# Attention scores from 128-row blocks that hold a head's high query rows over its low rows

## The chip, the cores and the metric

The kernel runs on one core of one Trainium2 chip. A run's time is the device time of one execution in microseconds (us). The engines are named as in the profile: PE is the matrix engine (PEld its weight loads), DVE the vector engine, ACT the scalar engine, POOL the general engine, SP the one that issues most transfers.

## What is computed

Two layers, each of three steps with a layer norm behind every one: a gated feed-forward step, a mixer, and a second gated feed-forward step. Sequence 256, width 1024. The mixer of layer 0 is an mLSTM, that of layer 1 windowed attention with 16 query heads of 64 columns, 4 key heads, a distance bias and a sink logit per head. The change touches the attention alone, of which the reference is (cut):

```python
def window_attention(x, w_in, sink, w_out):
    p = x @ w_in
    ...
    s = jnp.einsum('bnqkgd,bnskd->bnkgqs', q, kw).astype(jnp.float32) * (HEAD_DIM ** -0.5)
    ...
    s = s - slopes[:, :, None, None] * dist
    s = jnp.where(valid[None, :, None, None], s, MASK_VALUE)
    ...
    m = jnp.maximum(jnp.max(s, axis=-1, keepdims=True), sink_l)
    pe = jnp.exp(s - m)
    attn = pe / (jnp.sum(pe, axis=-1, keepdims=True) + jnp.exp(sink_l - m))
    o = jnp.einsum('bnkgqs,bnskd->bnqkgd', attn, vw.astype(jnp.float32)).reshape(B, S, nq)
    return o.astype(x.dtype) @ w_out
```

## The kernel before

Every product of float32 matrices is made from two parts of each operand: a high part that PE multiplies in its own format, and a low part, what the high part leaves over. ACT writes the high part (a copy or an activation with a scale), DVE subtracts it from the source and writes the low part; `split_evac` does both for what PE left in PSUM. A product then takes three matmuls, high by high, high by low and low by high, added up in PSUM (`mm3`). Weights come in pieces of 128 x 1024, each split in the same way into the rings `w_hi` and `w_lo` of 10 buffers.

Attention (`attn`) goes as follows. `proj` makes keys, values and the first half of the queries by token; `k_turn` and `q_turn` transpose them on PE and evacuate them into `kk` and `q2`. The second half of the queries comes out of `q_rest` already transposed, in four tiles, interleaved with the first scores. `kk` holds each key head twice, in partitions 0 to 63 and 64 to 127. `q2[:, j]` holds the pair j of heads, one head in partitions 0 to 63, the other in 64 to 127, and the third index chooses the high or the low part.

There are 8 pairs of heads. For each pair j, `scores` makes, per 128 tokens t, three products of 64 rows for each of the two heads, alternating between the heads and between two PSUM banks. DVE adds the distance bias and takes the row's maximum (the score reduction, a custom operation that the profile shows as CUSTOM_DVE_ANT_0 and an accumulator read, and the order as ISA), ACT takes the exponential and its sum, and POOL divides (`scale`). One step later PE transposes the probabilities and they are split (`turn`: pr0 and pr1), then multiplied with the values (`values`). There ACT copies one product to `o` and DVE adds the other, which lies in the other half of the partitions: `nc.vector.tensor_add(o[top], p[low, 0], o[top])`, and the same for `o[low]`. The sum is split into `q2[:, j]`, whose queries are no longer needed, and `out_proj` multiplies it with the output weights. All that is interleaved over 11 steps `st`.

What is executed when is not this code's order. Each engine call is only recorded (`Engine`), and `Program.issue` (the line that the profile gives for nearly every instruction) emits the records in the order of a table of numbers, `ORDER`: each number is the distance to the next record. A second table, `SLOTS`, says which of its buffers each tile takes. Each engine works through its own instructions strictly in the order in which they are emitted.

Of the kernel before, what the change touches and what calls it, by code (L numbers as in the profile page):

```python
# [264 lines left out]
        "365018925167"),  # L265
    "t.0": ("10423251205145435305135232350"),
    "stats": ("101001110110"),
    "mv": ("011010011101"),
    "rs": ("100011011011"),
    "raw.1": ("12301301302312032103102130302130"),  # L270
    "wt.1": ("3210"),
# [165 lines left out]
def trunk_kernel(ctx: ExitStack, tc: tile.TileContext, x, ffn_w_in, ffn_w_out, ln_g, ln_b, ml_w_in, ml_gate_b,  # L437
                 ml_norm_g, ml_w_out, at_w_in, at_sink, at_w_out, out):
    nc = Program(tc.nc)
# [1047 lines left out]
```

## Time and profile before

| | us |
|---|---|
| three runs | 914.37, 915.44, 916.11 |
| median | 915.44 |
| span of the profiled execution, first to last instruction | 914.3 |
| first start of a score matmul | 670.1 |
| last start of a score matmul | 709.8 |

The profile gives the span alone of the execution that it took; it lies 1.1 us under the median of the runs and 0.1 under the fastest. Of the whole span, the scores of all heads take 39.7 us. A row of a view names the line, the engine, the operation, and what it writes and reads (output <- inputs, buffer numbers left out). `fp32r` is the format of the high and low parts. The timeline gives the start, the time from there to the end, and how many neighbours of one kind were put together (x2). On PE the instructions overlap: what one costs is the step to the next start.

### The profile page before, as it was taken

The page shows a single profiled execution, that of the slowest core. Times are in us where ns is not written, and L with a number is a line of the kernel's source. Part 1 is how long each engine was busy: PE and PEld are TensorE (multiplying, and loading weights), DVE is VectorE, ACT ScalarE, POOL GpSimd, SP SyncE. Part 2 cuts the span into 40 slices and gives each one's busy share as a digit, 9 for nine tenths or more (in the row PEclk, how much of TensorE's full clock was granted, in tenths as well). Part 3 has the DMA queues.
Part 4 walks back from the last instruction along what each step waited for, and adds up shares of the span by engine and source line. Part 5 has one row for each costly group of instructions (what it writes and reads, how often), then busy time and mean ns, then how long its engine had stood idle before and what let it go on. Part 6 is the DMA issues. An engine that isn't in the chain of part 4 may idle for free.

```text
span 914.3 us, 12376 instructions
## 1 busy us (share of the span) xinstructions
PE 903.8 (99%) x4382; PEld 748.2 (82%) x4382; DVE 812.8 (89%) x987; ACT 576.8 (63%) x796; POOL 156.8 (17%) x200
## 2 busy tenths in 40 slices
PE   9999999999999999999999999999999999999996
PEld 7888888889988888887888888888887788888885
DVE  6998989997798999888999988899899899988897
ACT  6667567557655677565747666666488557666560
POOL 0211112113311121111012111120435311202110
PEclk9999999999999999999999999999999999999999
DMA  9999889558273889898957899987543396997971
GB/s 334 299 298 298 246 248 240 180 179 263 94 260 114 270 252 256 269 280 197 341 196 188 229 277 296 277 178 259 173 173 116 116 277 166 257 303 174 321 182 46
DMA packets 100670, 208.52 MB, mean 228 GB/s; under 512 B 6872, under 2 KB 21232, under 8 KB 100608
## 3 DMA queue, kind: packets, MB, share of 16 engines
q1 hardware_dynamic: 82832, 173.83, 54.1%
q0 software_dynamic: 17632, 33.64, 22.4%
q8 instruction: 34, 0.56, 0.2%
q10 hardware_dynamic: 144, 0.26, 0.1%
q14 instruction: 28, 0.23, 0.1%
HBM read 206.65 MB, written 1.05 MB: 227 GB/s over the span
## 4 chain that ended last, share of the span: by engine, by line
PE 96%; DMA 2%; DVE 1%; issue 1%; ACT 0%; DVEq 0%; POOL 0%; POOLq 0%
PE p L317 96%; DMA s_raw<-in_ffn_w_in_dram 1%; DMA ln_g<-in_ln_g_dram 1%; DVE w_lo L317 0%; DVE x L317 0%; ACT w_hi L317 0%; DVE h_lor L317 0%; DVEq L1483 0%; DVE hc_lor L317 0%; DVE t L317 0%; ACT xT_hi L317 0%; DVE stats L317 0%; DVE mv L317 0%; POOL ji L317 0%; DVE ident L317 0%
## 5 line engine op out<-in xcount | busy, mean ns | idle before, releaser
L317 ACT CAST w_hi<-s_raw 128x1024 fp32r<-128x1024 f32 x239 | 244.5, 1051 | 94.5 <-PE p L317 56.4
L317 DVE TENSOR_TENSOR w_lo<-s_raw,w_hi 128x1024 fp32r<-128x1024 f32 x239 | 285.6, 1218 | 19.6 <-ACT w_hi L317 15.6
L317 ACT CAST w_hi<-w_raw 128x1024 fp32r<-128x1024 f32 (+1 forms) x167 | 172.1, 1041 | 77.9 <-PE p L317 37.6
L317 DVE TENSOR_TENSOR w_lo<-w_raw,w_hi 128x1024 fp32r<-128x1024 f32 (+1 forms) x167 | 199.8, 1208 | 14.5 <-ACT w_hi L317 13.3
L317 PE MATMUL p<-w_hi,xT_hi 128*128 128x512 f32 x512 | 191.9, 394 | 0.8 <-ACT w_hi L317 0.5
L317 PE MATMUL p<-w_lo,xT_hi 128*128 128x512 f32 x512 | 192.1, 394 | 0.0
L317 PE MATMUL p<-w_hi,xT_lo 128*128 128x512 f32 x512 | 191.3, 394 | 0.0
L317 PE MATMUL p<-w_hi,h_lor 128*128 128x512 f32 (+1 forms) x323 | 119.9, 390 | 0.1
L317 PE MATMUL p<-w_hi,h_hir 128*128 128x512 f32 (+1 forms) x323 | 119.5, 391 | 0.0
L317 PE MATMUL p<-w_lo,h_hir 128*128 128x512 f32 (+1 forms) x323 | 118.6, 389 | 0.0
L317 PEld LDWEIGHTS p<-w_hi,xT_hi 128*128 128x128 f32 x512 | 95.8, 188 | 20.4 <-ACT w_hi L317 1.0
L317 PEld LDWEIGHTS p<-w_lo,xT_hi 128*128 128x128 f32 x512 | 96.0, 188 | 19.5 <-DVE w_lo L317 0.4
L317 PEld LDWEIGHTS p<-w_hi,xT_lo 128*128 128x128 f32 x512 | 96.1, 188 | 19.3 <-DVE xT_lo L317 0.3
L317 POOL DMA_DIRECT2D s_raw<-in_ffn_w_in_dram x43 | 52.2, 1266 | 329.0 <-DVE w_lo L317 90.5
L317 PE MATMUL p<-w_hi,S_hir 128*128 128x512 f32 x256 | 96.9, 390 | 0.0
L317 PE MATMUL p<-w_hi,S_lor 128*128 128x512 f32 x256 | 96.8, 390 | 0.0
L317 PE MATMUL p<-w_lo,S_hir 128*128 128x512 f32 x256 | 96.8, 390 | 0.0
L317 PEld LDWEIGHTS p<-w_hi,h_lor 128*128 128x128 f32 x323 | 60.6, 188 | 12.6 <-DVE h_lor L317 0.5
L317 PEld LDWEIGHTS p<-w_lo,h_hir 128*128 128x128 f32 x323 | 60.7, 188 | 12.2
L317 PEld LDWEIGHTS p<-w_hi,h_hir 128*128 128x128 f32 x323 | 60.5, 188 | 12.3 <-ACT h_hir L317 0.2
L317 PEld LDWEIGHTS p<-w_hi,S_hir 128*128 128x128 f32 x256 | 48.0, 188 | 10.5 <-ACT t L317 0.4
L317 PEld LDWEIGHTS p<-w_lo,S_hir 128*128 128x128 f32 x256 | 48.1, 188 | 10.1 <-DVE w_lo L317 0.2
(187 smaller groups left out, 1176.7 us busy)
## 6 DMA issues: line engine op xcount, KB each, us to landing
s_raw<-in_ffn_w_in_dram SPq DMA_DIRECT2D x101, 512.0 KB, 6.0
w_raw<-in_ffn_w_in_dram SPq DMA_DIRECT2D x58, 512.0 KB, 6.3
s_raw<-in_ffn_w_out_dram SPq DMA_DIRECT2D x55, 512.0 KB, 5.8
s_raw<-in_ffn_w_in_dram POOLq DMA_DIRECT2D x43, 512.0 KB, 7.1
w_raw<-in_ffn_w_out_dram SPq DMA_DIRECT2D x33, 512.0 KB, 7.1
w_raw<-in_ml_w_in_dram SPq DMA_DIRECT2D x24, 512.0 KB, 5.2
w_raw<-in_ffn_w_in_dram POOLq DMA_DIRECT2D x21, 512.0 KB, 7.8
s_raw<-in_ffn_w_in_dram SPq DMA_DIRECT2D x20, 256.0 KB, 6.1
```

The lines of the kernel that those rows point to most:

```text
L317: f(*args, **kw)
```

## The change

The layout of `q2` is different. `q2[0:64, j, a]` now holds the high part of the head a of pair j, and `q2[64:128, j, a]` its low part: the high rows stand over the low rows. As `kk` holds each key head twice, one matmul of 128 rows with the high keys makes high by high and low by high at once, and one with the low keys high by low and low by low. A head and 128 tokens take two matmuls of 128 rows in place of three of 64 rows, and the product of the two low parts is now added too. Over 8 pairs, 2 heads and 2 halves of the tokens that is 64 matmuls in place of 96.

The evacuation of the queries is made per head, so that each of the six (two in `q_turn`, four in `q_rest`) is two of 64 partitions on ACT and two on DVE, where it was one of 128 on each. Half of them write other partitions than they read.

```diff
             def q_turn(t):
...
-                split_evac((q2[:, 0:4, 0, tok(t)], q2[:, 0:4, 1, tok(t)]), p)
+                for a in range(2):
+                    split_evac((q2[0:64, 0:4, a, tok(t)], q2[64:128, 0:4, a, tok(t)]), p[64 * a:64 * a + 64])
...
             def q_rest(part):
...
-                        split_evac((q2[:, j, 0], q2[:, j, 1]), p, qs_col[:, j - 4:j - 3])
+                        for a in range(2):
+                            r = slice(64 * a, 64 * a + 64)
+                            split_evac((q2[0:64, j, a], q2[64:128, j, a]), p[r], qs_col[r, j - 4:j - 3])
...
             def scores(j, between):
...
                 for t in range(2):
-                    for n_, (qe, ke) in enumerate(((0, 0), (0, 1), (1, 0))):
-                        for a in range(2):
-                            r = slice(64 * a, 64 * a + 64)
-                            nc.tensor.matmul(ps[a][:, t], q2[r, j, qe, tok(t)], kk[ke][r, g], start=n_ == 0, stop=n_ == 2)
+                    for a in range(2):
+                        for e in range(2):
+                            nc.tensor.matmul(ps[a][:, t], q2[:, j, a, tok(t)], kk[e][:, g], start=e == 0, stop=e == 1)
```

Only these places of the code are new, but the tables `ORDER` (6654 records before, 6634 now) and most of `SLOTS` are new throughout:

```diff
-    "0 10 -9 8 2 -9 11 -10 11 15 1 -26 11 1 -11 12 1 -12 13 12 -24 13 1 11 -10 1 1 1 1 1 8 -7 17 -37 28 10 1 72 "
...
-    "sc.4": ("4245315103514231504321"),
+    "sc.4": ("0152153014253012543012"),
```

Counted over the records that both versions have, the place of an instruction in its engine's order moves by 3 on PE in the median and by 64 at most; 599 of 949 on DVE stay at the same place, and none moves by more than 11.

PE's order at the scores of the last pair of heads, before (p is a PSUM bank, kk the keys, q2r the queries or, behind them, the attention's output, pr the probabilities, v the values, w the output weights):

```order
L317 MATMUL p4_92<-w_hi4_72,q2r_4_0_238 128x512
L317 MATMUL p6_94<-kk_hir_4_0_227,q2r_4_0_238 128x256
L317 MATMUL p7_95<-kk_hir_4_0_227,q2r_4_0_238 128x256
L317 MATMUL p6_94<-kk_lor_4_0_228,q2r_4_0_238 128x256
L317 MATMUL p6_94<-kk_hir_4_0_227,q2r_4_0_238 128x256
L317 MATMUL p7_95<-kk_lor_4_0_228,q2r_4_0_238 128x256
L317 MATMUL p7_95<-kk_hir_4_0_227,q2r_4_0_238 128x256
L317 MATMUL p3_91<-w_hi9_77,q2r_4_0_238 128x512
```

And now, at the same pair:

```order
L312 MATMUL p6_94<-w_hi5_73,q2r_4_0_238 128x512
L312 MATMUL p0_88<-kk_hir_4_0_227,q2r_4_0_238 128x256
L312 MATMUL p5_93<-pr0_hir_4_1_250,v0r_4_0_236 128x512
L312 MATMUL p0_88<-kk_lor_4_0_228,q2r_4_0_238 128x256
L312 MATMUL p0_88<-kk_hir_4_0_227,q2r_4_0_238 128x256
L312 MATMUL p0_88<-kk_lor_4_0_228,q2r_4_0_238 128x256
L312 MATMUL p5_93<-pr1_hir_4_0_253,v1r_4_0_237 128x512
```

Six matmuls of 64 rows that stood in one block, two banks in turn, have become pairs of one bank that other matmuls are put between.

DVE's order at two evacuations of `q_rest`, before (sc are the scores, o and pr as above, w_lo a weight's low part):

```order
L317 TENSOR_TENSOR pr1_lor_4_1_256<-p1_89,pr1_hir_4_1_254 128x512
L317 SCALAR_TENSOR_TENSOR q2r_4_0_238<-p6_94,qs_col_4_0_226,q2r_4_0_238 128x256
L317 SCALAR_TENSOR_TENSOR q2r_4_0_238<-p4_92,qs_col_4_0_226,q2r_4_0_238 128x256
L317 TENSOR_TENSOR o_4_0_257<-p0_88,o_4_0_257 64x256 x2
L317 ISA sc_4_4_233,nm_4_1_242<-p4_92,dist_4_0_235,neg_sink_151 128x256
```

And now, at the last of the four:

```order
L312 TENSOR_TENSOR pr1_lor_4_1_256<-p7_95,pr1_hir_4_0_253 128x512
L312 TENSOR_TENSOR w_lo5_83<-w_raw3_67,w_hi7_75 128x1024
L312 SCALAR_TENSOR_TENSOR q2r_4_0_238<-p6_94,qs_col_4_0_226,q2r_4_0_238 64x256 x2
L312 TENSOR_TENSOR q2r_4_0_238<-o_4_0_257,q2r_4_0_238 128x256
L312 TENSOR_TENSOR o_4_1_258<-p4_92,o_4_1_258 64x256 x2
```

Where one instruction evacuated a tile of queries, two stand next to each other (x2), of 64 partitions each.

More of the change, by code (lines that the diff above doesn't have):

```diff
@@ L39 @@
 ORDER = (
[208 rows of a table removed]
[205 rows of a table added]
 )
 SLOTS = {
-    "raw.0": ("210375894260ab315798a1b2380476593806142893750a61b4735a0286b12a940280"),
-    "p": ("3015273416371651624740737037743003470071732475045321703262751465120457615023462034756305172461503713"
-        "6442055504252022042555024574651034561742340220420324423044423643153426021762340152301647420765314722"
-        "060227602276670206205326743621306753342132312243113214236"),
+    "raw.0": ("9173029854a76b31208961b439750a28397a1549830276a1b50326749ab146857497"),
+    "p": ("4026415701530160147372353253735225372270652373467520345212370617024673107425612456371547012610547317"
+        "2006455540656466406555461530231470520316714664164761167411175403560345135274032105612704420351674033"
+        "253025252003523053231625460452037610045200520045225024057"),
@@ L254 @@
     "h_hir.0": ("01001"),
     "h_lor.0": ("10101"),
-    "w_hi": ("1536089427819056375820935612483172106249564780132954061782549302675180974325916874210359678241306597"
-        "8240637195824063718459026378591430268719546372150862437689061249085367241903758623104975268413908217"
-        "5469870321659748031256784901375628147093568273041695371208346897520134659782013465920871649356809217"
-        "5368049215063874921506387491206537891234706592318672398160257386541934670253891457260389415762058963"
-        "905268715496"),
@@ L261 @@
-    "w_lo": ("8138121742486951046580796125370164658235182350986541234970895268317504678250734095386210549378012564"
-        "3185206793418250671824930568271469351690561739512805381576130867846245869374921053769842501271093864"
-        "2053149782160345781269073541976208452176048318292137523486914603568274168732498103528769175083257419"
-        "2653801479153869204715368940125739846550169834160253046821795345869732804613859740863742798750286574"
-        "365018925167"),
-    "t.0": ("10423251205145435305135232350"),
@@ L267 @@
-    "stats": ("101001110110"),
-    "mv": ("011010011101"),
-    "rs": ("100011011011"),
+    "w_hi": ("0256910247150936873149083654218574596420362719584032965714320894673519072843956173450829671435806279"
+        "1430689752143068971325046891257380461975236894720164389615067435012869437508921648703592461078531479"
+        "2065193847625901387426910537892641709358261492307658297431206159843720685914372068543197605286135479"
+        "0261385094367129504836712954036872154079236850741620781463082716894579623087154982063715948260391567"
+        "539061249856"),
@@ new lines @@
+    "w_lo": ("3137121482876951086570496125340168657235172350967581238940695276314508746250438695307216589340612578"
+        "3105249673810254961028734590261897351974591637512046301659134095189286197358720463597182640250473198"
+        "2460387512394086513297450683759241862359481031272305620869738940196258391502871340621597356410285637"
+        "4902185379246501387924506134872951630224801653804728430678912532601957643085621934805937918924780293"
+        "582460172689"),
+    "t.0": ("10423251205115035305430232305"),
@@ L270 @@
+    "stats": ("101001000010"),
+    "mv": ("011010001101"),
+    "rs": ("000011010100"),
     "raw.1": ("12301301302312032103102130302130"),
-    "wt.1": ("3210"),
+    "wt.1": ("2310"),
     "a_hir.1": ("1010"),
-    "a_lor.1": ("0101"),
     "den.1": ("1000"),
@@ L276 @@
     "hmv.1": ("0110"),
-    "hrs.1": ("1010"),
-    "h_hir.2": ("0111001001"),
+    "h_hir.2": ("1001001010"),
     "h_lor.2": ("1010110101"),
     "raw.2": ("8974561237058a96142b96a485712380b57326451983b70a26890ab75124a736b74912386b504896312b50a736271085b4a8"
-        "10954573b16809a2546289310a5b06741329"),
-    "t.2": ("0522403125023501514432433105224023511145331025223353143455"),
-    "sc.4": ("4245315103514231504321"),
-    "raw.4": ("14301534402132530145"),
-    "nm.4": ("22010202"),
-    "sm.4": ("10221202"),
-    "pr0_hir.4": ("00100110"),
-    "pr0_lor.4": ("11101011"),
-    "pr1_hir.4": ("10010010"),
-    "pr1_lor.4": ("11000000"),
-    "o.4": ("00001101"),
+        "109545a3b168097254628931075b764a1329"),
+    "t.2": ("0522403145203521514430433125004203511145331205003353143455"),
+    "sc.4": ("0152153014253012543012"),
+    "raw.4": ("14301534402132530154"),
+    "nm.4": ("20211110"),
+    "sm.4": ("01202102"),
+    "pr0_hir.4": ("00011101"),
+    "pr0_lor.4": ("01010111"),
+    "pr1_hir.4": ("10010110"),
+    "pr1_lor.4": ("11101101"),
+    "o.4": ("01010010"),
     "h_hir.5": ("10101"),
     "h_lor.5": ("10110"),
-    "raw.5": ("301302356a48159237091238b9ba560b79a208614b557a9328069b1a37a14a542813"),
-    "t.5": ("22311504210332350204153145144"),
+    "raw.5": ("30210325864015392b7a19203a365873ba6970814355b6a29078a3162b6146549012"),
+    "t.5": ("22411042514335304542103120512"),
 }
```

412 rows, old and new, of the table ORDER are left out of this document.

## The prediction, made before the changed kernel ran

> **What bounds the kernel now.** I read the page first, then TensorE's own waits, then the stretch of the score matmuls. The page's busy line and its chain of the work that ended last:
>
> ```profile
> PE 903.8 (99%) x4382; PEld 748.2 (82%) x4382; DVE 812.8 (89%) x987; ACT 576.8 (63%) x796; POOL 156.8 (17%) x200
> PE 96%; DMA 2%; DVE 1%; issue 1%; ACT 0%; DVEq 0%; POOL 0%; POOLq 0%
> ```
>
> PE works through 99% of the span, and the chain lies on it for 96%. What PE waits for (line, engine waited for, us in all, times, longest):
>
> ```profile
> PE p L317 <- DVE ident L317: 1.7, 1, 1.7
> PE p L317 <- ACT w_hi L317: 0.5, 1, 0.5
> PE p L317 <- DVE t L317: 0.3, 1, 0.3
> ```
>
> That is 2.5 us, 1.7 of it ahead of the first instruction. So a matmul removed shortens the span by its whole step, until another engine is late. The candidate is the vector engine, DVE. The windows from the first score matmul to the end of the last one, and from the first score reduction to the end of the last one (columns: length, PE, PEld, DVE, ACT, POOL busy, clock, DMA share, GB/s):
>
> ```profile
> 670.07:709.80 39.73, 39.73 (x277) 31.10 (x278) 36.20 (x97) 33.70 (x93) 23.27 (x47) 1.00 0.32 105
> 670.83:711.04 40.21, 40.21 (x277) 31.36 (x276) 36.86 (x100) 34.94 (x98) 24.51 (x51) 1.00 0.30 96
> ```
>
> PE is full at a clock of 1.00, DVE has 3.35 us free (40.21 less 36.86), ACT 5.3. The DMA engines are busy three tenths of the time: they set nothing here.
>
> **What the removed matmuls cost.** Their rows in the view of the query tile, and one of the 16 blocks of six in the timeline:
>
> ```profile
> L317 PE MATMUL p<-kk_hir,q2r x64: 273/333/389, 670.1 to 709.8; 64*128 64x256 f32 x64
> L317 PE MATMUL p<-kk_lor,q2r x32: 275/278/383, 670.3 to 709.7; 64*128 64x256 f32 x32
> ```
> ```profile
> 676.90 0.28 PE L317 MATMUL p<-xT_hi,w_lo 128*128 128x256 f32 x1
> 677.02 0.28 PE L317 MATMUL p<-xT_lo,w_hi 128*128 128x256 f32 x1
> 677.23 0.39 PE L317 MATMUL p<-kk_hir,q2r 64*128 64x256 f32 x2
> 677.45 0.28 PE L317 MATMUL p<-kk_lor,q2r 64*128 64x256 f32 x2
> 677.57 0.28 PE L317 MATMUL p<-kk_hir,q2r 64*128 64x256 f32 x2
> 677.78 0.39 PE L317 MATMUL p<-xT_hi,w_hi 128*128 128x256 f32 x1
> 678.00 0.28 PE L317 MATMUL p<-xT_hi,w_lo 128*128 128x256 f32 x1
> 678.12 0.29 PE L317 MATMUL p<-xT_lo,w_hi 128*128 128x256 f32 x1
> ```
>
> The durations overlap, so a matmul is priced by the step from its start to the next start. A 128-row matmul of 256 columns steps on after 0.12 (676.90 to 677.02, 678.00 to 678.12). The three pairs of 64-row matmuls start pairwise (x2 in 0.28 is hardly longer than one), but around them steps of 0.21 and 0.22 stand where 0.12 would: into the pairs, after the first pair, out of them, and after the first full matmul. From 677.02 to 678.00 is 0.98; less two ordinary steps of 0.12, the six cost **0.74**, not three steps of 0.12. Between matmuls of 512 columns it is the same:
>
> ```profile
> 701.50 0.39 PE L317 MATMUL p<-pr_hir,v0r 128*128 128x512 f32 x1
> 701.73 0.40 PE L317 MATMUL p<-w_hi,q2r 128*128 128x512 f32 x1
> ...
> 702.60 0.50 PE L317 MATMUL p<-w_hi,q2r 128*128 128x512 f32 x1
> 702.94 0.60 PE L317 MATMUL p<-ident,sc 128*128 128x128 f32 x4
> ```
>
> 701.73 to 702.94 is 1.21, less two steps of 0.23: 0.75. Sixteen blocks at 0.75 are 12.0. Two blocks are cut in two by other matmuls and pay twice; the piece of two at 684.77 in
>
> ```profile
> 684.48 0.36 PE L317 MATMUL p<-xT_hi,w_hi 128*128 128x256 f32 x1
> 685.21 0.38 PE L317 MATMUL p<-xT_lo,w_hi 128*128 128x256 f32 x1
> 685.43 0.28 PE L317 MATMUL p<-xT_hi,w_lo 128*128 128x256 f32 x1
> ```
>
> costs 0.95 less 0.24, or 0.71, so each cut adds some 0.65: 1.3. Together 13.3 us. The change puts 64 matmuls of 128 rows and 256 columns there, at 0.12: 7.7. **PE saves 5.6 us.**
>
> The Trainium skill, TensorEngine Tiling (Array Packing), speaks against the change: its section Theoretical Speedup gives up to 2x for a contraction of 64 or less. By that alone six would cost 0.36, four full ones 0.48, and the change would add 16 times 0.12. Its section Key Properties says, too, that changing the tiling mode drains the engine; the rows with 0.21 and 0.22 agree with that, and no run here has pairs without such a change.
>
> **What the change adds.** Each of the six evacuations of queries is now two on ACT and two on DVE, on 64 partitions, as wide as before. DVE's rows in its stretch, and ACT's around the stage:
>
> ```profile
> L317 DVE TENSOR_TENSOR pr_lor<-p,pr_hir 128x512 fp32r<-128x512 f32 x11 | 7.6, 687 | 1.0 <-ACT pr_hir L317 1.0
> L317 DVE TENSOR_TENSOR o<-p,o 64x256 f32<-64x256 f32 x8 | 3.4, 422 | 0.9 <-ACT o L317 0.7
> L317 DVE SCALAR_TENSOR_TENSOR q2r<-p,qs_col,q2r 128x256 fp32r<-128x256 f32 x4 | 1.8, 480 | 0.2 <-ACT q2r L317 0.2
> L317 DVE TENSOR_TENSOR q2r<-p,q2r 128x512 fp32r<-128x512 f32 x1 | 0.7, 691 | 0.1
> L317 ACT ACTIVATE q2r<-p,qs_col 128x256 fp32r<-128x256 f32 x4 | 1.8, 462 | 0.0
> L317 ACT CAST q2r<-p 128x512 fp32r<-128x512 f32 x2 | 1.2, 583 | 1.6 <-PE p L317 1.6
> ```
>
> 64 partitions take as long as 128 (422 ns for o, 418 for q2r<-o of the same width), so DVE gets 4 x 0.48 + 2 x 0.69 = 3.3 and ACT 4 x 0.46 + 2 x 0.58 = 3.0. ACT's lies in its 5.3 us free. Counted in the new order, DVE has 75 instructions beside the accumulator reads from the first score reduction to the last, where it had 69: four more of 0.48, one of 0.69, two o of 0.42, one pr_lor less: +2.8, of which back-to-back overlap (some 0.08 each) takes back 0.5. So 36.86 becomes **39.1**. PE in the same stretch has 5.6 less, but eleven more matmuls of 256 columns, three of 512, a transpose more and one of 512 less: 11 x 0.12 + 2 x 0.23 + 0.1 = 1.9. So 39.73 becomes **36.0**. DVE's stretch is 0.5 longer than PE's for the same work: 38.6 against 36.0. PE must wait at least **2.6 us** for DVE, whose results the transposes, the value matmuls and the next banks need; behind a waiting PE stand only PE's own later matmuls.
>
> One more price is not shown on the new instructions. The pair of q2r is printed as 0.87 for x2, the pair of o as 0.86:
>
> ```profile
> 683.88 0.87 DVE L317 SCALAR_TENSOR_TENSOR q2r<-p,qs_col,q2r 128x256 fp32r<-128x256 f32 x2
> 685.43 0.86 DVE L317 TENSOR_TENSOR o<-p,o 64x256 f32<-64x256 f32 x2 [0.68 <-ACT o L317]
> ```
>
> Two q2r of 0.48 overlap by 0.09; two o of 0.42 don't overlap at all, and o is what writes other partitions than its neighbour. The new low parts write partitions 64 to 127 from 0 to 63, between instructions that write from 0. If each loses the overlap ahead, between and behind, that is 0.25 a pair and 1.2 for the five pairs in the stretch. The bounds are 0 and 1.2; I take 1.2, since o is the nearest row.
>
> The Trainium skill, VectorE: DVE Perf Modes, section Two Vector instructions with no wait between them, says that an instruction is held until all earlier ones have finished if an input or its output starts in another quadrant of partitions than the one before; the o row agrees, and by it the sum holds the whole 1.2.
>
> So PE waits 2.6 + 1.2 = 3.8 of the 5.6: **net -1.8**. The span of 914.3 becomes 912.5; the median of the runs, 915.44, lies 1.1 above the span, and by the same difference the time is **913.6**. The two q_turn pairs ahead of the first score I cost at nothing beside this: projection matmuls stand there on PE. If that cover fails, each is late by 0.58 + 0.69. The tables of order and slots are new in the other stages too; there PE waits 0.8 us now after its start, so they have little to win, and I give them 1 us either way.
>
> **The rivals.** A difference under 0.2%, 1.8 us, can't be told from none.
>
> Forecast, chance 0.60: DVE becomes the bound of the stretch and gives back about two thirds. From 912.4 (no lost overlap) to 915.3 (lost overlap, and half of the 3.35 us idle kept). Half of it lies beyond the 0.2%.
>
> PE keeps nearly all, 0.20: DVE's surplus is put off past the last score, where its results are needed later. Price: 0 to 1.9 us of waits, 909.8 to 911.7, likeliest 910.8. For it: DVE may lag by as many buffers as there are. Against it: the 75 instructions stand in the stretch by order.
>
> Slower, 0.13: DVE keeps its 3.35 us idle, since they are answers from ACT (1.0 for pr_hir, 0.7 for o above) and PE, not slack. Then PE waits 2.6 + 1.2 + 3.35 = 7.2, and 5.6 is overdrawn by 1.6: 917.0. It decides from 1.8 us of such idle time on; 0.09 of it lies beyond the 0.2%. Against it: an engine with a full queue waits less.
>
> The change doesn't do what it says, 0.04: full matmuls with a weight load each (182 ns and more) step by 0.19 instead of 0.12, PE saves 13.3 - 12.2 = 1.1, and nothing waits: 914.3. Against it the rows at 0.12, each with its own load.
>
> The pairs were cheaper than I read, 0.03: if the steps of 0.21 and 0.22 stay with the neighbours after the change, six matmuls cost 3 x 0.12 and four cost 4 x 0.12, the change adds 16 x 0.12 = 1.9, and the time is 917.3. Against it: no pair of 128-row matmuls in the rows above shows such a step away from the 64-row ones. The Trainium skill's factor of 2x, cited above from TensorEngine Tiling (Array Packing), would give this case.
>
> Faster: 0.30 + 0.20 = 0.50. Slower: 0.09 + 0.03 + 0.01 for the rest of the order = 0.13. Within: 0.37. The range, 910.0 to 917.0, leaves out the best of the second case and the worst of the third and the last.
>
> **What would show it.** The score rows turn into 64 of 128x256 with steps of 0.12 to their neighbours. In the stretch of the scores, PE's busy time falls under the window's length by about 4 us, waiting for DVE's pr_lor, o, q2r or sc; DVE's goes above 95%. The pair of q2r is printed as 0.96 or more where 0.87 stands. If PE shows no wait there, the second case holds; if DVE is idle for 2 us or more and PE with it, the third; if the steps are 0.19, the fourth. A stall of PE in another stage would make the whole sum wrong, since it looks at this stretch alone.

## The result and the profile after

| | time, us (median) | ratio to before | span, us |
|---|---|---|---|
| before, in the same comparison | 915.78 (4 runs) | | 914.3 |
| after | 924.73 (4 runs) | 1.0094 [1.0075, 1.0114] | 923.1 |

The change makes the kernel slower by 8.9 us; 913.6 was predicted, and 917.0 was the upper end of the range. The medians in this document are over all executions of a run, and a few of these stand far above the rest: without one each, of 1951, 1128 and 1290 us, the runs called e3, e4 and e14 below have 919.77, 921.97 and 925.13, and e3's trace, taken of the 1951, is not read. The page of after, its busy line and its chain of the work that ended last:

```profile
PE 905.8 (98%) x4350; PEld 748.5 (81%) x4350; DVE 817.6 (89%) x993; ACT 577.5 (63%) x802; POOL 151.0 (16%) x200
PE 77%; DVE 9%; DMA 6%; issue 3%; ACT 3%; SPq 1%; DVEq 0%; ACTq 0%
```

The chain lay on PE for 96% and now for 77%; the rest is DVE, ACT and loads. What PE waits for in after, beside the 1.7 us ahead of its first instruction (engine waited for, us in all, times, longest):

```profile
PE p L312 <- DVE pr_lor L312: 1.5, 2, 1.1
PE p L312 <- DVE t L312: 1.5, 2, 1.0
PE p L312 <- ACT w_hi L312: 0.9, 1, 0.9
PE p L312 <- ACT a_hir L312: 0.8, 1, 0.8
PE p L312 <- DVE h_lor L312: 0.8, 2, 0.6
PE p L312 <- DVE o L312: 0.7, 1, 0.7
```

Only pr_lor and o belong to attention. t, w_hi, a_hir and h_lor are names of the stages whose code is unchanged. So the loss has two places, and the windows size them. From 20 to 330 and from 330 to 655 us, all ahead of attention, first of before, then of after (columns as in the prediction):

```profile
20.00:330.00 310.00, 310.00 (x1559) 261.96 (x1558) 277.81 (x344) 198.60 (x277) 53.53 (x60) 1.00 0.77 230
330.00:655.00 325.00, 324.59 (x1478) 266.17 (x1478) 293.61 (x306) 201.06 (x240) 49.41 (x58) 1.00 0.85 248
```
```profile
20.00:330.00 310.00, 309.18 (x1551) 260.38 (x1550) 275.37 (x341) 194.29 (x272) 49.88 (x60) 1.00 0.76 227
330.00:655.00 325.00, 321.57 (x1455) 262.15 (x1454) 291.54 (x303) 202.56 (x242) 39.48 (x51) 1.00 0.85 249
```

In the same time PE does 8 and 23 matmuls fewer. At 325 / 1478 = 0.22 us a matmul that is 6.8 us in this trace before attention has begun, and 2.1 remain. The stretch of attention from the first score reduction to the last, of after:

```profile
677.60:719.50 41.90, 39.20 (x254) 33.06 (x253) 40.70 (x106) 38.38 (x105) 24.25 (x46) 1.00 0.25 84
```

It was 40.21 us long and is 41.90. The last matmul of the attention's output with the weights starts at 738.9 us, in before at 730.7: 8.2 late. So attention costs about 1.5 us, where I forecast a gain of 1.8, and the stages behind it, whose code is unchanged too, the rest, about 0.7. DVE is busy for 97% of the stretch and PE falls 2.7 under its length; these are signs that I had named for the forecast case (above 95%, about 4).

### The profile page after: what moved, and what is told of

Read it like the earlier page. It is cut to its first block, busy times and chain, and to the rows that moved or that the text cites. A ratio compares the mean times of both kernels' runs of the same rounds, so it can differ in the third digit from the quotient of the medians.

```text
span 923.1 us, 12289 instructions
## 1 busy us (share of the span) xinstructions
PE 905.8 (98%) x4350; PEld 748.5 (81%) x4350; DVE 817.6 (89%) x993; ACT 577.5 (63%) x802; POOL 151.0 (16%) x200
## 4 chain that ended last, share of the span: by engine, by line
PE 77%; DVE 9%; DMA 6%; issue 3%; ACT 3%; SPq 1%; DVEq 0%; ACTq 0%
PE p L312 77%; DVE w_lo L312 5%; DMA s_raw<-in_ffn_w_in_dram 2%; ACT w_hi L312 2%; DMA w_raw<-in_ml_w_in_dram 2%; DMA s_raw<-in_ffn_w_out_dram 1%; DVE sc L312 1%; DMA w_raw<-in_ffn_w_in_dram 1%; DMA x<-in_x_dram 1%; DVE pr_lor L312 1%; SPq L312 1%; DVE q2r L312 1%; DVE o L312 1%; DVE t L312 0%; ACT wt L312 0%
## 5 line engine op out<-in xcount | busy, mean ns | idle before, releaser
L312 DVE TENSOR_TENSOR w_lo<-s_raw,w_hi 128x1024 fp32r<-128x1024 f32 (+1 forms) x242 | 288.9, 1217 | 27.7 <-ACT w_hi L312 23.3
L312 ACT CAST w_hi<-s_raw 128x1024 fp32r<-128x1024 f32 (+1 forms) x242 | 246.2, 1048 | 94.1 <-PE p L312 39.9
L312 DVE TENSOR_TENSOR w_lo<-w_raw,w_hi 128x1024 fp32r<-128x1024 f32 (+1 forms) x164 | 197.3, 1218 | 15.3 <-ACT w_hi L312 12.9
L312 ACT CAST w_hi<-w_raw 128x1024 fp32r<-128x1024 f32 (+1 forms) x164 | 169.0, 1046 | 66.4 <-PE p L312 35.4
L312 PE MATMUL p<-w_hi,xT_hi 128*128 128x512 f32 x512 | 196.1, 396 | 1.6 <-DVE t L312 1.5
L312 PE MATMUL p<-w_lo,xT_hi 128*128 128x512 f32 x512 | 195.1, 394 | 0.0
L312 PE MATMUL p<-w_hi,xT_lo 128*128 128x512 f32 x512 | 194.5, 394 | 0.0
L312 PE MATMUL p<-w_lo,h_hir 128*128 128x512 f32 (+1 forms) x323 | 121.0, 391 | 0.0
L312 PE MATMUL p<-w_hi,S_hir 128*128 128x512 f32 x256 | 98.8, 393 | 1.3 <-ACT w_hi L312 0.9
```

The source lines that it names most:

```text
L312: f(*args, **kw)
```

## The experiments

Each time is set beside runs of the kernel before on the same chip in the same session, and a difference in us is one of medians, to those runs. "Of before" and "of after" mean the code, or the tables ORDER and SLOTS, of that kernel.

### Where the loss arises

**New code, old order (e1).** After's code; the tables of before, with

```
- six 64-row matmuls per block, two parts per evacuation
+ each head's two 128-row matmuls where its last of three stood
+ an evacuation's two parts on ACT where its one stood, the same on DVE
```

> The new score matmuls and the new evacuations stand in the order and the slots of before: each head's two matmuls where its last of three stood, the four parts of an evacuation where its two stood. All other instructions stand as before. Theory A (the new order of the other stages makes the loss; of the 9 us, 6.5 arise before the attention stage): the time is at or below before's 915.4, between 909.8 (PE keeps 5.6) and 915.5. Rival B (the new code makes attention itself slower, whatever the order): 917 or more, with PE's new waits in the score stretch only. Rival C (a score matmul of 128 rows steps by 0.19 or more): 914 to 916, with steps of 0.19 in the timeline.

Measured: 919.13, 1.0039 [1.0027, 1.0051]. It loses 3.3, so the tables carry the other 5.6 us of the 8.9. That is a balance: by the trace of after they lose about 7.5 outside attention, and in attention the new order costs this code about 1.5 where before's order costs it 3.3. The same windows of this run show that PE is on time ahead of attention (1559 and 1480 matmuls):

```profile
330.00:655.00 325.00, 324.72 (x1480) 266.28 (x1479) 294.13 (x306) 201.53 (x240) 49.43 (x58) 1.00 0.85 249
```

Theory A's bound of 915.5 falls too: in before's order the new code costs 3.3 us, nearly all in the score stretch, so B holds for that part. The stretch of the reductions is 3.1 us longer than before, with DVE idle for 3.5 of it:

```profile
671.60:714.90 43.30, 38.19 (x249) 32.62 (x248) 39.82 (x105) 37.95 (x103) 24.39 (x50) 1.00 0.26 83
```

The steps of 0.19 aren't there.

**Old code, new order (e2).** Before's code, tables of after, the six matmuls together where the last of the four stood.

> The code of before in the order and the slots of after: the six 64-row matmuls stand together where the last of the four stood, the two parts of an evacuation where the second pair of the four stood. Theory A: the loss of the other stages stays, 6 to 7 us ahead of attention, so 921 to 924, and 4 to 7 us of stalls of PE outside the score stretch. Rival B: the loss goes with the code, 914 to 917.

Measured: 927.06, 1.0123 [1.0109, 1.0138]: the loss stays without the new code. It is 3 us above the 921 to 924 that Theory A expected; that an order laid out for four matmuls loses more with six is my reading, not shown. In the two windows its trace has 1558 and 1455 matmuls. So the 23 missing from 330 to 655 us, 5.1 us, come again with the tables, and most of the 8 missing before 330 us don't (1559 in before; 1556 in e14 and e18, which have after's tables there): they seem to belong to the one execution of after that was traced.

**Two hybrids (e3, e4).**

```
e3: code of after;  tables of after from 655 to 738 us, of before elsewhere
e4: code of before; tables of before from 655 to 738 us, of after elsewhere
```

> The new code; order and slots of after from 655 to 738 us (the attention stage), of before everywhere else. Theory A (the new order of the other stages costs 6.5 us, attention in its own new order 2): 917 to 919, with PE's waits on pr_lor and o in the score stretch and none of the long ones at 239, 416, 430 and 533 us. Rival B (the loss is all the new code's and comes with its order in attention): 922 or more.

> The code of before; order and slots of before from 655 to 738 us, of after everywhere else. Theory A: 921 to 923, PE about 6.5 us late when attention begins, nothing lost in it. Rival B: 915 to 917.

Measured: e3 920.03, 1.0052 [1.0039, 1.0065]; e4 922.47, 1.0068 [1.0052, 1.0084]. By time both side with the tables of the other stages, but neither is clean. e3 loses some 4 us and not 2. e4 has the time of Theory A without its reason: PE was to be 6.5 us late when attention begins, and it is on time, with 1559 and 1478 matmuls in the two windows.

```profile
330.00:655.00 325.00, 324.35 (x1478) 266.31 (x1477) 294.19 (x307) 200.32 (x240) 47.06 (x58) 1.00 0.85 250
```

Yet up to 649 us PE, ACT and DVE carry out the same operations in the same order as in after, by the tiles' names with the two kinds of load buffer, `s_raw` and `w_raw`, taken as one. It differs there mainly in which of these buffers the loads take (from the seventh entry of the string `raw.2` of `SLOTS` on) and the place of a few load issues. So the new order of the engines doesn't stall PE by itself: with loads in other buffers it runs on time. Of the 7.0 us that e4's span is longer, 5.4 arise behind attention; its largest wait of PE is at 781 us, where after has none, and again a late load stands ahead of it on ACT:

```profile
PE p L303 <- DVE t L303: 2.8, 2, 2.3
777.89 2.00 ACT L303 CAST w_hi<-s_raw 128x1024 fp32r<-128x1024 f32 x2 [4.15 <-DMA s_raw<-in_ffn_w_in_dram]
```

Near the seams, too, loads are issued in another sequence than in either kernel. I rest the split between attention and the rest on e1 and the windows above.

### Why attention gains nothing

**The matmuls alone (e5)**, before's order:

```
-  for n_, (qe, ke) in enumerate(((0, 0), (0, 1), (1, 0))): for a in range(2): ... matmul of 64 rows
+  for a in range(2): for e in range(2): matmul(ps[a][:, t], q2[:, j, a, tok(t)], kk[e][:, g], ...)
```

> Before's order and evacuations; only the score matmuls become four of 128 rows (their product mixes the two heads of a pair, since the layout of the queries is before's: part of the computation is changed). DVE gets nothing to do. If the matmuls save 5.6 us of PE and DVE is no bound: 909.8. If DVE's stretch bounds PE by what I read (PE 39.7 less 5.6 is 34.1 against DVE's 36.9 busy): PE waits 2.8 or more, 912.6 or less saved. If the 64-row pairs are as cheap as three steps of 0.12: 917.3.

Measured: 914.79, 0.9990 [0.9981, 0.9998]. PE's own work shrank as forecast: in after's timeline 128-row score matmuls step on after 0.12 like their neighbours,

```profile
690.41 0.28 PE L312 MATMUL p<-xT_hi,w_hi 128*128 128x256 f32 x1
690.53 0.28 PE L312 MATMUL p<-kk_lor,q2r 128*128 128x256 f32 x1
690.65 0.28 PE L312 MATMUL p<-kk_hir,q2r 128*128 128x256 f32 x1
690.77 0.28 PE L312 MATMUL p<-kk_lor,q2r 128*128 128x256 f32 x1
```

but only 1.0 of 5.6 us arrives. The reductions' stretch in e5:

```profile
671.10:710.10 39.00, 37.80 (x249) 32.43 (x248) 36.62 (x100) 35.09 (x98) 26.17 (x50) 1.00 0.32 97
```

PE has idle time now and the stretch is 1.2 shorter. So PE's full stretch was no bound from which all of its saving could be had.

**Less for DVE (e0, e8, e9).** Before, e1 and e5 without the two lines `nc.vector.tensor_add(o[...], p[...], o[...])`.

> Before, without the two additions per pair that DVE makes into o (half of the values left out): the base for the two runs that leave them out. PE is full in the stretch, so 914.5 to 915.6 by every theory. Below 914.5, part of the 2 us that the matmuls alone gained without those additions is theirs.

> The matmuls alone (as in the run of that name, with its mixed scores), without the two additions per pair into o (half of the values left out): 6.7 us less for DVE. If DVE's busy time took back what the matmuls save: 910 to 911.5, PE free of waits in the score stretch. If the 128-row matmuls save less than the 5.6 us that I read: 913 or more, with no waits of PE there.

> The new code in the order of before, without the two additions per pair that DVE makes into o (half of each head's values is left out of the sum): 16 x 0.42 = 6.7 us less work for DVE, PE and ACT unchanged. If DVE's busy time is what takes the saving back and more: 912 to 914, and PE's waits on q2r shrink with DVE's. If it is the length of the chain from q_rest over ACT and DVE to the next scores: PE still waits 3 us or more for q2r, 917 to 919.

Measured: e0 915.84, 0.9999 [0.9990, 1.0008]; e9 913.54, 0.9980 [0.9971, 0.9988]; e8 918.45, 1.0032 [1.0020, 1.0045]. Of the saved 5.6, DVE's work took back 1.1 (2.1 arrive in e9, 1.0 in e5). Another 3.5 don't come even with DVE idle for 5.1 of 38.5 us there:

```profile
670.80:709.30 38.50, 37.32 (x248) 32.13 (x247) 33.43 (x90) 34.59 (x98) 27.00 (x50) 1.00 0.31 102
```

I expected 910 to 911.5 there, wrongly: DVE's sum doesn't bound this stretch in before's order. That the way of a result through DVE, ACT and POOL back to PE does is what these runs leave as a reading; PE's named waits in e9 are too short (1.2 us after its start) to show it. And e8 loses almost what e1 does (2.8 and 3.3); its line on q2r reads as e1's:

```profile
PE p L316 <- DVE q2r L316: 4.6, 4, 1.6
```

**The 64-row blocks joined (e13).** Before, on PE only:

```
- block of 128 tokens t = 0 ... other matmuls ... block t = 1
+ block t = 0, block t = 1 ... other matmuls        (seven of eight pairs of heads)
```

> Before, with only the order of PE changed: the six 64-row matmuls of a pair's second 128 tokens follow directly on those of the first (seven pairs of heads; the two blocks that were cut are whole). No work is added or removed. If the steps of 0.2 around 64-row matmuls are paid once a run, as I read them: seven times some 0.38 and two cuts of 0.65, 4.0 us less: 911.5 to 913. If what binds the stretch are the chains over DVE and ACT: 915 to 916, with new waits of PE in it.

Measured: 916.11, 1.0003 [0.9993, 1.0012]. One joined block, the six pairs in five rows:

```profile
685.48 0.28 PE L306 MATMUL p<-xT_hi,w_lo 128*128 128x256 f32 x1
685.69 0.39 PE L306 MATMUL p<-kk_hir,q2r 64*128 64x256 f32 x2
685.91 0.28 PE L306 MATMUL p<-kk_lor,q2r 64*128 64x256 f32 x2
686.03 0.40 PE L306 MATMUL p<-kk_hir,q2r 64*128 64x256 f32 x4
686.27 0.28 PE L306 MATMUL p<-kk_lor,q2r 64*128 64x256 f32 x2
686.39 0.28 PE L306 MATMUL p<-kk_hir,q2r 64*128 64x256 f32 x2
686.60 0.66 PE L306 MATMUL p<-ident,sc 128*128 128x128 f32 x4
```

685.48 to 686.60 is 1.12; less one ordinary step of 0.12, twelve matmuls cost 1.00, where two separate blocks cost 1.5. The steps of 0.2 stand at the edges (into the run, behind its first pair, out of it); inside, a pair starts every 0.12 (686.27 to 686.39). The Trainium skill, TensorEngine Tiling (Array Packing), section Theoretical Speedup, gives up to 2x for such pairs, and inside the run the trace agrees. By the prices of the prediction PE has some 4 us less to do (an estimate), and the time is the same. So a second saving, made in another way and without a new instruction, brings nothing; PE's work alone doesn't set the time of this stage. The change moves the scores as well, though: PE waits 1.4 us for pr_lor in this trace, where before has no such wait, so part of a saving may be lost to the move.

**The evacuations alone (e6)**, before's order and matmuls:

```
-  split_evac((q2[:, j, 0], q2[:, j, 1]), p, ...)
+  for a in range(2): split_evac((q2[0:64, j, a], q2[64:128, j, a]), p[r], ...)
```

> Before's order and its six 64-row matmuls per block; only the six evacuations of queries are cut in two, the low parts written to the other half of the partitions (so the scores are products of other rows than the reference's: part of the computation is changed). If ACT and DVE have room for it: 915.4 to 915.9. If the lost overlap is what reaches PE: 916.6 (1.2 for five pairs). If all of the added DVE time does: 918.7 (3.3 us). The spacing of the q2r pair's starts is 0.4 before; with the hold it is 0.48 or more.

Measured: 919.70, 1.0044 [1.0032, 1.0056]: 3.9 us, more than all the DVE time added. Less the 1.0 of e5 that is 2.9 of the 3.3 in e1. One evacuation of q_rest in before, then in e6:

```profile
678.79 0.45 ACT L317 ACTIVATE q2r<-p,qs_col 128x256 fp32r<-128x256 f32 x1
679.28 0.48 DVE L317 SCALAR_TENSOR_TENSOR q2r<-p,qs_col,q2r 128x256 fp32r<-128x256 f32 x1 [0.17 <-ACT q2r L317]
```
```profile
680.52 0.95 ACT L318 ACTIVATE q2r<-p,qs_col 64x256 fp32r<-64x256 f32 x2
681.50 1.00 DVE L318 SCALAR_TENSOR_TENSOR q2r<-p,qs_col,q2r 64x256 fp32r<-64x256 f32 x2 [0.66 <-ACT q2r L318]
682.65 1.07 PE L318 MATMUL p<-ident,sc 128*128 128x128 f32 x8 [0.91 <-DVE q2r L318]
```

Before: 678.79 to 679.76, 0.97. In e6: 680.52 to 682.50, 1.98. DVE doesn't start when the first high part is done (680.52 + 0.47), but when both are, though it has been idle for 0.66. The other sequence takes turns as well. In after's first evacuation of q_turn high and low parts alternate, and ACT's second high part waits 0.76 for DVE's first low part, of which it needs nothing:

```profile
666.83 0.58 ACT L312 CAST q2r<-p 64x512 fp32r<-64x512 f32 x1
667.44 0.69 DVE L312 TENSOR_TENSOR q2r<-p,q2r 64x512 fp32r<-64x512 f32 x1 [0.50 <-ACT q2r L312]
668.17 0.58 ACT L312 CAST q2r<-p 64x512 fp32r<-64x512 f32 x1 [0.76 <-DVE q2r L312]
```

Why they wait is open: both engines read one PSUM bank and write one tile, and no run separates the two. PE then waits for q2r, 2.3 us in all in e6's trace. The Trainium skill, PSUM — Partial Sum Buffer, section PSUM bank collisions raise a hardware error, says that two engines may use one bank at once in different quadrants, and calls guarding by bank the simple version; by that ACT on partitions 64 to 127 and DVE on 0 to 63 need not wait for the bank. No run here shows it; it wasn't tried.

**The chain, the work and the crossing apart (e10, e12).** Both in before's order, layout and matmuls:

```
e10: + nc.scalar.activation(q2[:, j, 0], p, AF.Copy, ...)     the high part written twice, the same in q_turn
e12: + for r in (slice(0, 64), slice(64, 128)): split_evac((q2[r, j, 0], q2[r, j, 1]), p[r], ...)
```

> Before, with the high part of each of the six evacuations of queries written twice by ACT (the same values): the chain from PE over ACT and DVE to the next scores is 0.46 or 0.58 us longer, DVE's work and every output are as before. Theory L (the length of that chain is what costs in the evacuations alone, where it was 0.95 or 1.27 us longer and the time 4 us): 917 to 918, PE waiting for q2r. Rival W (DVE's added work or its writes to the other partitions cost it): 915.4 to 916.

> Before, with each of the six evacuations of queries cut in two 64-partition parts that stay in their own partitions: as many instructions as in the evacuations alone, no write to the other half of the partitions, and before's layout and result. Theory L: as slow as the evacuations alone, 919 to 920. Rival W with the crossing as its cause (0.25 a pair and 1.2 in all were predicted): 1.2 or more below the evacuations alone, 918.5 or less, and the pair of DVE's q2r takes 0.87 to 0.90 instead of 1.00.

Measured: e10 918.03, 1.0021 [1.0012, 1.0030]; e12 919.62, 1.0046 [1.0033, 1.0058]. Theory L in both. e10 adds nothing to DVE, only 4 x 0.46 + 2 x 0.58 = 3.0 us of length to the six chains, and costs 2.2. (ACT's work grows by the same 3.0; and the sign that I had named, PE waiting for q2r, is weak, 0.5 us in its trace.) e12 costs as much as e6 though it writes nowhere else than before; its pair takes as long as the crossing one:

```profile
680.89 1.00 DVE L318 SCALAR_TENSOR_TENSOR q2r<-p,qs_col,q2r 64x256 fp32r<-64x256 f32 x2 [0.67 <-ACT q2r L318]
```

So the lost overlap (1.00 instead of 0.87) is real and belongs to the pair on different halves, whether it crosses or not, and the crossing costs nothing. What the lost overlap itself costs is not shown, since both runs have it; DVE's 3.3 us of added work can't be much of the 3.9, since e8 relieves DVE of 6.7 and gets 0.5 back.

**Can the chain be covered? (e15)** e1 with

```
- score block or transposes that wait for q2r; 8 to 13 ready matmuls
+ 8 to 13 ready matmuls; score block or transposes          (three places)
```

> The new code in the order of before, with three groups of PE put off by some 1.2 us: the second score block of the first pair, the eight transposes and the score block that waited 1.6, 1.2 and 1.05 us for q2r stand behind 8 to 13 matmuls that were ready. Theory L (the longer chain of the evacuations is what costs, and it can be covered): 915.5 to 917. If DVE's added time bounds the stretch: 918.5 or more, with the waits moved to pr_lor, o or sc.

Measured: 920.13, 1.0054 [1.0041, 1.0067]. PE's waits for q2r fall from 4.6 to 0.7 us, and others take their place, in e15's waits of PE:

```profile
PE p L303 <- DVE nm L303: 3.0, 3, 1.6
PE p L303 <- DVE pr_lor L303: 1.7, 2, 1.2
```

That is the outcome expected of the rival, DVE's added time as the bound; e8 speaks against it, and DVE is idle for 4.9 of 44.6 us here, so the run doesn't decide. My reading is that scores that come later make their banks free later (nm) and their probabilities late (pr_lor); at any rate the chain wasn't covered by putting off its consumers. In after's own order it is: PE has no wait for q2r there of 0.2 us or more, and DVE, not idle as in e1, is busy for 97%. Whether DVE's sum is the bound in that order is open: no run relieves DVE in it.

### Why the stages with unchanged code lose

Following PE's largest stalls in after back by what each instruction waited for gives one picture. At 533 us (ACT and PE rows):

```profile
532.77 1.05 ACT L312 CAST w_hi<-s_raw 128x1024 fp32r<-128x1024 f32 x1 [2.54 <-DMA s_raw<-in_ffn_w_out_dram]
533.73 1.98 ACT L312 CAST w_hi<-w_raw 128x1024 fp32r<-128x1024 f32 x2
534.81 0.74 PE L312 MATMUL p<-w_hi,S_hir 128*128 128x512 f32 x2 [0.90 <-ACT w_hi L312]
```

ACT stands 2.54 us before a load that isn't there, with two splits behind it whose loads are, and PE waits for the first of these. At 416 us it is DVE, with t behind the late load and PE behind t:

```profile
416.03 1.23 DVE L312 TENSOR_TENSOR s_raw<-s_raw,s_raw 128x1024 f32<-128x1024 f32 x1 [1.77 <-DMA s_raw<-in_ffn_w_in_dram]
417.17 0.68 DVE L312 TENSOR_TENSOR t<-t,p 128x512 f32<-128x512 f32 x1
417.91 0.50 PE L312 MATMUL p<-w_hi,xT_hi 128*128 128x512 f32 x1 [1.04 <-DVE t L312]
```

**Four moves (e14)** in after:

```
DVE  - weight add or split (1.22); t or h_lor       + t or h_lor; weight add or split     (416, 430, 572 us)
ACT  - high part with the late load; two others     + two others; high part with the late load   (533 us)
```

> After, with four moves outside attention on DVE and ACT: at 416, 430 and 572 us a weight's add or split (1.22 us each) goes behind the small results of the tokens (t, h_lor) that PE waits for, and at 533 us the split of w_hi0, which waits 2.5 us for its load, goes behind two splits whose loads have landed. Theory A in its last form (the new order of the other stages puts work that PE waits for behind weight work, some of it with a late load, on engines that work strictly in order): PE's stalls at 416, 430, 533, 537 and 572 (4.0 us in all) shrink, 920.5 to 922.5. Rival B2 (the loss there is spread or moves on to the next place): 923.5 or more.

Measured: 925.72, 1.0117 [1.0099, 1.0136], nothing gained. At 533 us I had moved the high part and left its low part where it stood on DVE, ahead of h_lor. The wait went from one queue to the other:

```profile
532.57 1.23 DVE L301 TENSOR_TENSOR w_lo<-s_raw,w_hi 128x1024 fp32r<-128x1024 f32 x1 [2.84 <-ACT w_hi L301]
535.59 0.50 PE L301 MATMUL p<-w_hi,h_lor 128*128 128x512 f32 x1 [1.47 <-DVE h_lor L301]
```

**Two places in full (e18)**: the move at 416, and at 533 the high part as in e14 and its low part behind h_lor.

> After, with two places mended in full: at 416 us the sum with the late load behind t as in the run with four moves, and at 533 us both halves of the late weight moved, its high part on ACT behind two high parts whose loads have landed and its low part on DVE behind h_lor (the run with four moves had left the low part where it was, and DVE idled 2.84 us for it). Theory A: the stalls of 1.2, 1.07 and 0.37 us go and nothing comes in their place, 922 to 923. Rival B2 (the time is lost again further on, since DVE and the loads have no slack there): 924 or more, with as many matmuls from 330 to 655 us as in after.

Measured: 921.73, 1.0071 [1.0052, 1.0090]; 3.0 us are back by the medians, 2.1 by the ratios (whose intervals overlap between 1.0075 and 1.0090), and both stalls are gone. PE does 12 of the 23 missing matmuls again:

```profile
330.00:655.00 325.00, 324.05 (x1467) 264.35 (x1467) 293.86 (x307) 201.31 (x240) 43.37 (x56) 1.00 0.85 250
```

The trace is of the fastest of six executions, 1.7 us under the median, so the 12 may be a little flattered. So two such places are about half of what is lost here; the 11 matmuls still missing, 2.4 us, were not shown place by place. Such a place takes two things, work that PE waits for behind weight work, and a load that is late. e18 takes away the first; e4 keeps the order and takes away the second: at the place of 416 us DVE waits 1.15 for the load instead of 1.77 and PE 0.42 for t instead of 1.04, at that of 533 neither ACT nor PE waits, and PE is on time. Which of the changed buffers makes the loads late in after is not shown.

**One move in before (e17)**, the same remedy at the same place (a load 2.3 us late at 413 us):

```
DVE  - s_raw + s_raw; w_lo; t; hc_lor      + t; hc_lor; s_raw + s_raw; w_lo
```

> Before, with one move on DVE: at 413 us the sum of two loaded pieces, whose load lands 2.3 us late, and the split behind it stand after the two results of tokens (t, hc_lor) that PE waits for. Theory A: PE's two stalls there, 0.8 us, go: 914.8 to 915.2. Else 915.5 or more.

Measured: 917.20, 1.0022 [1.0013, 1.0032], 2.0 us slower instead of faster. DVE idles there all the same, 1.93 for the product that t needs instead of 2.3 for the load; the two weight instructions come later, and the next t is late by more than was won:

```profile
413.28 0.69 DVE L306 TENSOR_TENSOR t<-t,p 128x512 f32<-128x512 f32 x1 [1.93 <-PE p L306]
420.18 0.44 PE L306 MATMUL p<-ident,t 128*128 128x128 f32 x2 [1.27 <-DVE t L306]
```

DVE is busy for 293.61 of 325 us there, so weight work put off at one place is late at the next. A stall in the trace is not yet a gain to be had.

Of the versions that do the whole computation none was faster than the kernel before; e5 and e9, which were, leave part of it out.

## Why the prediction was wrong, by its steps

**PE's saving (5.6)** was right as work: steps of 0.12, and the joined blocks show that the 0.2 steps are paid at the edges. The rivals with steps of 0.19 and with cheap pairs fall.

**PE as the bound of the score stretch** was the wrong reading of 99%. I took it that a matmul removed shortens the span until DVE is late, gave DVE 2.6 us, and left 3.0. e5 shows 1.0, e13 nothing, e9 2.1 with DVE relieved: PE was full, and something beside it was nearly as long. That it is the chain of results is the reading that fits, not shown by itself.

**The evacuations** failed in their kind. I priced them as busy time: ACT's "lies in its 5.3 us free", and "The two q_turn pairs ahead of the first score I cost at nothing beside this". The price if that cover fails, 0.58 + 0.69, stood in the next sentence, and it failed. The largest single wait for q2r in e1 is that of q_turn's second pair:

```profile
672.04 1.18 ACT L316 CAST q2r<-p 64x512 fp32r<-64x512 f32 x2 [1.38 <-PE p L316]
673.25 1.39 DVE L316 TENSOR_TENSOR q2r<-p,q2r 64x512 fp32r<-64x512 f32 x2 [0.77 <-ACT q2r L316]
674.79 0.36 PE L316 MATMUL p<-kk_hir,q2r 128*128 128x256 f32 x1 [1.60 <-DVE q2r L316]
```

Each chain is longer by 1.0 (q_rest, above) to 1.3 us (here 2.6 instead of 0.58 + 0.69), since both low parts start only after both high parts. In before's order that costs 3.9 us (e6), where I had counted 2.6 and 1.2 of DVE's time against a saving that doesn't arrive. In after's order PE doesn't wait for them.

**The lost overlap (1.2)**: the pair is as predicted, 0.98 in after where 0.87 stood. The crossing that I gave as its cause costs nothing of its own (e12 against e6). The Trainium skill, VectorE: DVE Perf Modes, section Two Vector instructions with no wait between them, holds an instruction whose input or output starts in another quadrant; e12's pair, in which inputs and output change together, agrees with 1.00. Whether the 1.2 was right as a term of the sum no run shows: none has the halves without the lost overlap.

**In attention together**, the 5.6 saved and about 1.5 more are given back in after, 7.1 us where I had 3.8; in before's order it is 8.9 (5.6 and the 3.3 of e1). The third rival gave 7.2, and 917.0; in after its amount is right, but its reason, that DVE keeps 3.35 us of idle time, holds in e1 (3.5) and not in after (1.2 of 41.90). I gave it 0.13. DVE's busy time in after, 40.70, is near what I had, 39.1 and the 1.2; the stretch is longer all the same, and what makes it so in that order is open.

**The other stages**: "there PE waits 0.8 us now after its start, so they have little to win, and I give them 1 us either way." This is the step that made most of the error: about 7.5 us by the trace of after, 5.6 net by e1; of it, the 5.1 from 330 to 655 us come again in e2. Little to win was right, and says nothing of what there is to lose: with DVE at 90% and loads at 0.85 of the DMA engines' time, a late load with work behind it that PE needs stops PE. I looked at the order and not at where the loads land, and e4 shows that the same order is on time with other buffers. The last sentence on what would show it named this case, and no rival had it.

## What to carry to other kernels

Where one engine is at 99% and the next at 92%, read the chain of results beside the busy times before pricing a saving: remove some of the full engine's work alone, and see what arrives. Price an added pair of instructions by what it adds to the way from producer to consumer, not by its engine's free time. And a table that fixes the order of everything is part of the change in every stage that it covers: its risk is what the queues there can lose, and it is tested by running the new code in the old order. Look at the buffers of the loads as well as at the order: a load that lands late stops whatever stands behind it.

## What was not expected of the hardware

64-row matmuls in a longer run keep their pairwise start: twelve in 1.00 us, with long steps only into the run, behind its first pair and out of it (e13).

An evacuation cut in two on ACT and DVE is twice as long from end to end, 1.98 instead of 0.97, though the engines are different and the halves independent: nothing of the second high part ran beside the first low part, in e6, where the high parts come first, or in after, where the parts alternate. What makes them take turns is open.
